# Two transformer blocks on one core: four edits to queues, buffers and engines at the seams between stages

## The chip, the core and the metric

The kernel runs on one core of one Trainium2 chip. Its engines have queues of their own, each worked off in order: TensorE (PE, the matmuls), VectorE (DVE), ScalarE (ACT), GpSimd (POOL) and SyncE (SP), which issues nearly all DMAs. The metric is the device time of one execution in microseconds (us), from the first instruction to the last.

## The reference

```python
def first_block(x, ...):                       # 1024 rows of 1024
    proj = rms_norm(x, norm1_g) @ w_in         # attention, convolution and pooling branches
    mix = concat([att(8 heads), conv, pool])
    x = x + mix @ w_out
    up = causal_depthwise_conv(rms_norm(x, norm2_g) @ w_up, ffn_dw_w)
    gate, val = split(up)                      # 2816 channels each
    return x + (silu(gate) * val) @ w_down

def second_block(x, ...):
    ...                                        # differential and neighbourhood attention, gates
    x = x + rmsnorm(merged @ w_out, post_mix_w)
    h = rmsnorm(x, pre_ffn_w)
    f = (silu(h @ w_gate) * (h @ w_up)) @ w_down
    return x + rmsnorm(f, post_ffn_w)

reference = second_block(first_block(x))       # all in float32
```

## The kernel before

All matmuls are float32 made from three passes: every operand is split into a high part (`hi`, a cast on ACT) and the rest (`lo`, a subtraction on DVE or POOL, `lo_of`), and a product is hi*hi + lo*hi + hi*lo. The feed-forward networks (FFN) use Strassen's scheme in a seven-product form. Going up (`ffn_up`), `T1` to `T7` are seven sums of quarters of the input, held in SBUF; each of 22 channel groups c has seven weight sums (A1 to A7) and seven products, whose PSUM tiles are named x, y and z. Channel groups come in pairs, and the seven sums of a finished pair are stored to DRAM (`gD`, 77 stores in each FFN). Going down (`ffn_down`), four groups of 2, 3, 3 and 3 pairs load these sums and the weight's quarters (11 loads of 256 KB for a pair), DVE makes the weight sums (L975), ACT and `lo_of` split (tiles `hl`), and seven products are added into eight rows.

The stages of the trace (us): the first mixing stage to about 474, `out1` (mix @ w_out) from 403 to 526, first way up 526 to 1012, first way down 1012 to 1240, second mixing stage, second `out` to 2192, second way up 2192 to 2656, second way down 2656 to 2886.

The code gives what is computed and from which buffers. The order on each engine comes from a list scheduler at build time with its own estimates of durations; a wait that turns out longer on the chip holds up all that stands behind it in that queue.

Places that the change touches. `attn_head` writes a head's output (`pvt`) to DRAM (`mixD`), and `out1` loads it back (`split_T`) and splits it as an operand `hA`, `hB`; the last pair of heads (`mixD[3]`) is read back last. The weights of `out1` (`wr<-in_w_out_dram`) and these loads share one tag of two buffers. In `ffn_up`, `weights_a` loads two 512 KB weight blocks for a channel group (tag `wr`, three buffers) and `weights_b` forms the other sums (`ws`); all split weights lie in tag `w`. `lo_of` gives a split to POOL and DVE in turn.

Of the kernel before, what the change touches and what calls it, by code (L numbers as in the profile page):

```python
# [11 lines left out]
F32R = mybir.dt.float32r  # L12
# [3 lines left out]
NOSYNC = mybir.DependencyInfo(mybir.DependencyClass.NoSync, mybir.DependencyReason.DATA)  # L16
# [4 lines left out]
P = 128  # L21
# [4 lines left out]
NF = DFF // P  # L26
# [55 lines left out]
class Net:  # L82
# [236 lines left out]

    def attn_head(self, st, V, lane, spans, in1, pool, ps, dst, causal=False):  # L320
        nc = self.nc
        for g in range(2):
            pv = ps.tile([P, 512], F32, tag="pv", name=self.n("pv"), bufs=1)
            for j in (2 * g, 2 * g + 1):
                ts = {}
                for qb in (2 * j, 2 * j + 1):
# [5 lines left out]
                    r = self.sm(1, "rs")  # L332
# [20 lines left out]
                for bk in banks:  # L353
# [13 lines left out]
                    for kb, qs in bk:  # L367
# [11 lines left out]
            nc.vector.tensor_tensor(out=tmp[lane:lane + 64, :], in0=pv[lane:lane + 64, :],  # L379
                                    in1=tmp[lane:lane + 64, :], op=ALU.add)  # L380
            nc.sync.dma_start(out=dst[lane:lane + 64, g * 512:(g + 1) * 512], in_=tmp[lane:lane + 64, :])

# [19 lines left out]
    def mix1(self, pb, pt):  # L402
# [17 lines left out]
        def att(pr, pb):  # L420
            for hh in range(2):
                h = 2 * pr + hh
                st = self.load_stacks(pb, qD[pr], kD[pr], hh * 64)
                V = pt.tile([P, NB, P], F32R, tag="V", name=self.n("V"))
                nc.sync.dma_start(out=V.bitcast(F32), in_=vD[h])
                cB = pb.tile([P, S], F32, tag="cB", name=self.n("cB"))
                nc.sync.dma_start(out=cB, in_=cumD[h].partition_broadcast(P))
                yield from self.attn_head(st, V, hh * 64, CAUSAL, lambda qb: lambda a, b: [(a, b, cB[:, a:b])],
                                          pt, ps, self.mixD[pr], True)

        gB = self.bcast_row(I["norm1_g"][0], pb, "cB", 2)
        with self.pool("p1a", side="right") as pa:
# [18 lines left out]
            for pr in range(4):  # L451
                f = chain(*fill[pr])
                for _ in att(pr, pb):
                    for _ in range(1):
                        next(f, None)
                    n += 1
                    while rate[pr] and n * rate[pr] >= 1:
                        n -= 1 / rate[pr]
                        next(bg, None)
                drain(f)  # L460
# [206 lines left out]
    def out1(self, rows, pp, done):  # L667

        nc, I = self.nc, self.I
        W = I["w_out"][0]  # L670
        mT = self.new_hT()
        ws = []
# [20 lines left out]
        for i in range(4):  # L693
            part(i, 1, w1[:6])
        self.split_T(self.mixD[3], mT, 3)
        gB, jk = (self.wpool.tile([P, D], F32, tag="wr", name=self.n("wr"), bufs=2) for _ in range(2))
# [70 lines left out]
    def ffn_up(self, T, fT, fw, R, ps, Wg, cg, Wu, cu, conv, gD, close_sums):  # L767
        nc = self.nc
        chans, raws, pts = {}, {}, {}
        G, V, b_ = R[0], R[1], R[2][:, :S]  # L770
        t1, t2, t3, s1, s2, s4 = (R[i][:, o:o + 512] for i, o in ((3, 0), (3, 512), (4, 0), (4, 512), (7, 0), (7, 512)))
# [3 lines left out]
        def split(raw, w):  # L775
            hi, lo = (fw.tile([P, 1024], F32R, tag="w", name=self.n("w"), bufs=11)[:, :w] for _ in range(2))
            nc.scalar.copy(out=hi, in_=raw)  # L777
            self.lo_of(lo, raw, hi)
            return [(hi[:, o:o + 512], lo[:, o:o + 512]) for o in range(0, w, 512)]

        def weights_a(c):

            r = [fw.tile([P, 2, 512], F32, tag="wr", name=self.n("wr"), bufs=3) for _ in range(2)]
            for t, W, col in ((r[0], Wg, cg + c * P), (r[1], Wu, cu + c * P)):
                nc.sync.dma_start(out=t.rearrange("p h (k m) -> p (h k) m", k=4),
                                  in_=W[:, col:col + P].rearrange("(k p) m -> p k m", p=P))
            A = chans[c] = {}
            A[1], A[2] = split(r[0].rearrange("p h x -> p (h x)"), 1024)
            raws[c] = r
# [56 lines left out]
        def finish(c):  # L846
# [15 lines left out]
            if c % 2:  # L862
                a11, a21, a12, a22 = gp[0][:, :512], gp[0][:, 512:], gp[1][:, :512], gp[1][:, 512:]
                nc.vector.tensor_tensor(out=s1, in0=a21, in1=a22, op=ALU.add)
                nc.vector.tensor_tensor(out=a21, in0=a11, in1=a21, op=ALU.subtract)
                nc.vector.tensor_tensor(out=s2, in0=s1, in1=a11, op=ALU.subtract)
                nc.vector.tensor_tensor(out=s4, in0=a12, in1=s2, op=ALU.subtract)
                for i, t in ((1, a11), (2, a12), (3, s4), (4, a22), (5, s1), (6, s2), (7, a21)):
                    nc.sync.dma_start(out=gD[c // 2, i - 1], in_=t)

        for c in (0, 1):
            weights_a(c)
        for i in (3, 4, 6, 7, 5):
# [67 lines left out]
    def ffn_down(self, acc, keep, gD, Wd, fx, fr, fh, ps, done):  # L941
# [16 lines left out]
        def load(ps_):  # L958
# [5 lines left out]
            for i, half in ((1, 0), (1, 1), (5, 0), (5, 1), (6, 0), (3, 1), (7, 0), (4, 0), (2, 1), (3, 0), (2, 0)):  # L964
                for p in ps_:
                    if half == 0:
                        nc.sync.dma_start(out=X[p][i][:, 0], in_=gD[p, i - 1])
                    else:
                        r, h = {1: (0, 0), 5: (0, 1), 3: (1, 1), 2: (1, 0)}[i]
                        r = (2 * p + r) * P  # L970
                        nc.sync.dma_start(out=X[p][i][:, 1], in_=Wd[r:r + P, h * 512:(h + 1) * 512])
            for p in ps_:
# [18 lines left out]
        assert p == np_  # L991
        loaded = load(groups[0])
        rest = list(range(NB)) if keep is not None else []
        for gi, grp in enumerate(groups):
# [4 lines left out]
            for i in DOWN:  # L999
                hl = []  # L1000
                for p in grp:
                    raw = loaded[p][i].rearrange("p a b -> p (a b)")
                    hi, lo = (fh.tile([P, 1024], F32R, tag="hl", name=self.n("hl"), bufs=12) for _ in range(2))
                    nc.scalar.copy(out=hi, in_=raw)  # L1004
                    self.lo_of(lo, raw, hi)
                    hl.append((hi, lo))
# [412 lines left out]
```

## Time and profile before

| | |
|---|---|
| time, median of 3 runs | 2899.86 us (2897.95 to 2903.76) |
| profiled execution | 2904.8 us, its span 2903.0 us |
| PE busy | 2709.1 us, 93% of the span |
| mean granted TensorE clock | 0.972 of full speed |
| DVE, ACT, POOL busy | 1791.7, 1195.8, 913.7 us |

Busy time is the union of an engine's instructions. PE carries the span; what it does not carry is waiting that lies at the seams between stages and once per channel group on the first way up. The clock is 1.0 at the higher of TensorE's two levels (2.4 GHz) and 0.5 at the lower (1.2 GHz).

### The profile page before, as it was taken

To read this page: it belongs to the slowest core of one execution; us is meant where nothing else is said; L and a number is where in the kernel's file an instruction comes from. 1 tells how busy PE (TensorE), PEld (TensorE's weight loads), DVE (VectorE), ACT (ScalarE), POOL (GpSimd) and SP (SyncE) were. 2 spreads that over 40 slices of the span, in tenths; PEclk is the share of its full clock that TensorE was granted. 3 is DMA by queue.
4 is the path that set the end of the run, shared out by engine and by line. 5 is a ranking of instruction groups with operands and counts; after the bars stand their busy time and mean duration, and the time that the engine had idled before them with its cause. 6 is when DMAs were issued, how large, how long until landed. Compare 5 with 4: busy or idle time off the path is not lost. (4 is left out here: it accounts for less than half of the span.)

```text
span 2903.0 us, 37142 instructions
## 1 busy us (share of the span) xinstructions
PE 2709.1 (93%) x13686; PEld 2265.8 (78%) x13686; DVE 1791.7 (62%) x2730; ACT 1195.8 (41%) x1879; POOL 913.7 (31%) x642
## 2 busy tenths in 40 slices
PE   7999898899999989999999999998997999998997
PEld 7799677677777768888888978886776788886786
DVE  4697664677776799845666533444427544555977
ACT  4344553344444443334445444544323433333333
POOL 3256431222222144531212253422422211123445
PEclk9999999999999989999999999999998999999999
DMA  5445451223322474155654394525422233336522
GB/s 167 132 119 145 130 189 64 80 73 102 98 96 86 141 264 157 46 193 157 174 159 124 106 225 128 138 81 170 143 90 87 79 103 106 105 102 222 204 87 97
DMA packets 318143, 375.08 MB, mean 129 GB/s; under 512 B 42692, under 2 KB 215168, under 8 KB 317448
## 3 DMA queue, kind: packets, MB, share of 16 engines
q1 hardware_dynamic: 317960, 372.70, 41.8%
q8 instruction: 108, 1.77, 0.3%
q14 instruction: 75, 0.61, 0.1%
HBM read 257.01 MB, written 115.61 MB: 128 GB/s over the span
## 5 line engine op out<-in xcount | busy, mean ns | idle before, releaser
L765 POOL TENSOR_TENSOR hl<-x,hl 128x1024 fp32r<-128x1024 f32 x77 | 220.1, 2873 | 270.1 <-ACT hl L1004 220.3
L139 POOL TENSOR_TENSOR wl<-wr,wh 128x1024 fp32r<-128x1024 f32 x73 | 186.6, 2558 | 349.7 <-ACT wh L138 314.9
L1004 ACT CAST hl<-x 128x1024 fp32r<-128x1024 f32 x154 | 153.1, 1049 | 230.1 <-PE x L118 127.0
L317 ACT ACTIVATE t<-t,mx 128x640 f32<-128x640 f32 (+3 forms) x192 | 172.8, 901 | 160.8 <-DVE mx L313 155.0
L118 PE MATMUL x<-hl,hl 128*128 128x512 f32 x704 | 218.0, 396 | 5.2 <-DVE hl L765 2.8
L765 POOL TENSOR_TENSOR w<-wr,w 128x1024 fp32r<-128x1024 f32 (+1 forms) x44 | 84.7, 1924 | 389.6 <-PE x L118 288.0
L118 PE MATMUL mm<-hA,wh 128*128 128x512 f32 x608 | 198.0, 400 | 4.6 <-ACT gs L1204 4.6
L765 POOL TENSOR_TENSOR w<-ws,w 128x1024 fp32r<-128x1024 f32 x44 | 107.8, 2450 | 298.1 <-issue 210.7
L118 PE MATMUL mm<-hB,wh 128*128 128x512 f32 x608 | 196.4, 397 | 1.0 <-ACT gs L1204 1.0
L118 PE MATMUL y<-hl,hl 128*128 128x512 f32 x528 | 167.6, 403 | 16.6 <-DVE hl L765 12.8
L365 DVE TENSOR_TENSOR pl<-tr,ph 128x512 fp32r<-128x512 f32 (+2 forms) x160 | 100.4, 634 | 123.1 <-DMA yD<-pvt 42.9
L334 POOL TENSOR_SCALAR t<-t,rs 128x640 f32<-128x640 f32 (+7 forms) x128 | 106.4, 838 | 204.8 <-DVE rs L333 175.1
L118 PE MATMUL mm<-wh,hB 128*128 128x256 f32 (+1 forms) x752 | 164.0, 306 | 4.1 <-ACT hB L180 4.1
L118 PEld LDWEIGHTS x<-hl,hl 128*128 128x128 f32 x704 | 134.3, 191 | 35.4 <-DVE hl L765 4.3
L118 PE MATMUL mm<-wh,hA 128*128 128x256 f32 (+1 forms) x704 | 150.7, 302 | 11.2 <-ACT hA L127 7.8
L777 ACT CAST w<-ws 128x1024 fp32r<-128x1024 f32 x88 | 92.6, 1053 | 127.3 <-PE x L118 103.3
L118 PE MATMUL x<-hl 128*128 128x512 f32 x352 | 137.1, 398 | 6.2 <-DVE r L985 6.1
L364 ACT CAST ph<-tr 128x512 fp32r<-128x512 f32 (+2 forms) x160 | 84.8, 542 | 139.1 <-PE tr L359 93.6
L118 PE MATMUL z<-T2h,w 128*128 128x512 f32 x352 | 120.0, 402 | 23.0 <-DVE r L814 21.3
L118 PEld LDWEIGHTS mm<-hA,wh 128*128 128x128 f32 x608 | 115.3, 191 | 29.1 <-ACT gs L1204 5.3
L118 PE MATMUL sc<-KH,QS 128*128 128x512 f32 (+1 forms) x320 | 125.9, 396 | 12.1 <-DVE mx L313 9.0
L765 DVE TENSOR_TENSOR hl<-x,hl 128x1024 fp32r<-128x1024 f32 x77 | 129.7, 1687 | 11.1 <-ACT hl L1004 10.8
(345 smaller groups left out, 7674.7 us busy)
## 6 DMA issues: line engine op xcount, KB each, us to landing
gD<-r SPq DMA_DIRECT2D x154, 256.0 KB, 2.5
x<-gD SPq DMA_DIRECT2D x154, 256.0 KB, 5.3
wr<-in_w_up_dram SPq DMA_DIRECT2D x66, 512.0 KB, 3.8
wr<-in_w_in_dram SPq DMA_DIRECT2D x50, 512.0 KB, 7.2
x<-in_w_down_dram SPq DMA_DIRECT2D x88, 256.0 KB, 3.8
wr<-in_w_gate_dram SPq DMA_DIRECT2D x22, 512.0 KB, 4.1
wr<-in_w_out_dram SPq DMA_DIRECT2D x16, 512.0 KB, 4.1
QS<-q2D SPq DMA_DIRECT2D x32, 256.0 KB, 5.4
```

The lines of the kernel that those rows point to most:

```text
L118: self.nc.tensor.matmul(out, lhsT, rhs, start=start, stop=stop, **kw)
L139: g = (lo_engine or nc.gpsimd).tensor_tensor(out=lo, in0=raw[:, :n], in1=hi.bitcast(F32), op=ALU.subtract)
L317: nc.scalar.activation(out=t[:, :nb * P], in_=t[:, :nb * P], func=AF.Exp, scale=-1.0, bias=m, accum_out=s)
L334: nc.gpsimd.tensor_scalar(out=t[:, :nb * P], in0=t[:, :nb * P], scalar1=r, scalar2=1.0, op0=ALU.mult, op1=ALU.mult)
L364: nc.scalar.copy(out=ph[:, :w], in_=tr[:, :w])
L365: nc.vector.tensor_tensor(out=pl[:, :w], in0=tr[:, :w], in1=ph[:, :w].bitcast(F32), op=ALU.subtract)
L765: return eng.tensor_tensor(out=lo, in0=raw, in1=hi.bitcast(F32), op=ALU.subtract)
L777: nc.scalar.copy(out=hi, in_=raw)
L1004: nc.scalar.copy(out=hi, in_=raw)
```

## The change

Five edits, the fourth of which isn't in its short name.

- The last pair of attention heads is not stored: `attn_head` splits its output straight into the operand `mT` (four splits of 64x512 on ACT and DVE in place of four stores, one load and a split of 128x1024). `mT` is allocated before that pair.
- The first two channel groups of each `ffn_up` load their weights from ACT's DMA queue, not SP's.
- The seven `gD` stores of the last pair are ordered behind the last weight load of the first way-down group (an order for the scheduler, not a wait).
- Tag `w` in `ffn_up` has 8 buffers, not 11.
- In the first way-down group, all `lo` splits go to DVE (`lo_of(..., 1)`), seven of them POOL's before.

```diff
-    def attn_head(self, st, V, lane, spans, in1, pool, ps, dst, causal=False):
+    def attn_head(self, st, V, lane, spans, in1, pool, ps, dst, causal=False, direct=None):
...
+            if direct is not None:
+                mT, k = direct
+                part = slice(lane, lane + 64)
+                self.split(tmp[part, :], mT[0][g][part, k, :], mT[1][g][part, k, :], nc.vector)
+                continue
             nc.sync.dma_start(out=dst[lane:lane + 64, g * 512:(g + 1) * 512], in_=tmp[lane:lane + 64, :])
...
-                                          pt, ps, self.mixD[pr], True)
+                                          pt, ps, self.mixD[pr], True, (self.mT, 3) if pr == 3 else None)
...
+                if pr == 3:
+                    self.mT = self.new_hT()
...
-        mT = self.new_hT()
+        mT = self.mT
...
-        self.split_T(self.mixD[3], mT, 3)
...
-            hi, lo = (fw.tile([P, 1024], F32R, tag="w", name=self.n("w"), bufs=11)[:, :w] for _ in range(2))
+            hi, lo = (fw.tile([P, 1024], F32R, tag="w", name=self.n("w"), bufs=8)[:, :w] for _ in range(2))
...
-        def weights_a(c):
+        def weights_a(c, queue=nc.sync):
...
-                    nc.sync.dma_start(out=gD[c // 2, i - 1], in_=t)
+                    d = nc.sync.dma_start(out=gD[c // 2, i - 1], in_=t)
+                    if c == NF - 1:
+                        self.late.append(d.ins)
...
         for c in (0, 1):
-            weights_a(c)
+            weights_a(c, nc.scalar)
...
-                        nc.sync.dma_start(out=X[p][i][:, 1], in_=Wd[r:r + P, h * 512:(h + 1) * 512])
+                        self.mark = nc.sync.dma_start(out=X[p][i][:, 1], in_=Wd[r:r + P, h * 512:(h + 1) * 512])
...
+        for ins in self.late:
+            self.tc.add_manual_dep(ins, self.mark.ins.name, NOSYNC, reason="late")
...
-                    self.lo_of(lo, raw, hi)
+                    self.lo_of(lo, raw, hi, 2 if gi else 1)
```

The scheduler answers these edits with new orders. Three places follow. First SP's queue at the end of the first attention, before (`wr` are weight blocks of `out1` or read-back parts of `mixD`, `r` the eight input rows of the residual):

```order
L663 DMA wr_4838<-mixD 128x1024
L135 DMA wr_4844<-in_w_out_dram 128x2x512
L381 DMA mixD<-pvt_4085 64x512
L572 DMA mixD<-mo_4015 128x512
L572 DMA mixD<-mo_4021 128x512
L425 DMA V_4525<-vD 128x1024
L381 DMA mixD<-pvt_4247 64x512
L572 DMA mixD<-mo_4027 128x512
L572 DMA mixD<-mo_4033 128x512
L663 DMA wr_4850<-mixD 128x1024
L663 DMA wr_4856<-mixD 128x1024
L678 DMA r_1041_4786<-in_x_dram 128x1024
```

The same place after the change; `wr_4848` is what `wr_4844` was, and `wr_4830` what was `wr_4826`, ten rows ahead of the first row above:

```order
L685 DMA r_1045_4794<-in_x_dram 128x1024
L685 DMA r_1046_4795<-in_x_dram 128x1024
L685 DMA r_1047_4796<-in_x_dram 128x1024
L685 DMA r_1048_4797<-in_x_dram 128x1024
L685 DMA r_1049_4798<-in_x_dram 128x1024
L685 DMA r_1050_4799<-in_x_dram 128x1024
L685 DMA r_1051_4800<-in_x_dram 128x1024
L685 DMA r_1052_4801<-in_x_dram 128x1024
L135 DMA wr_4830<-in_w_out_dram 128x2x512
L670 DMA wr_4836<-mixD 128x1024
L670 DMA wr_4842<-mixD 128x1024
L135 DMA wr_4848<-in_w_out_dram 128x2x512
```

The two weight blocks move from ahead of the last attention stores to behind the eight loads of 512 KB. The matmuls that need them move with them, from between the steps of the last heads to behind the last head.

Second, PE in the middle of the first way up (x, y, z are PSUM tiles, T1 to T7 the operands). Before, the product z of the next channel group begins between two others:

```order
L118 MATMUL y_6711<-T5h_5533,w_6697 128x512
L118 MATMUL y_6711<-T5l_5534,w_6697 128x512
L118 MATMUL y_6711<-T5h_5533,w_6698 128x512
L118 MATMUL z_6852<-T2h_4799,w_6828 128x512
L118 MATMUL z_6852<-T2l_4800,w_6828 128x512
L118 MATMUL x_6712<-T6h_5529,w_6697 128x512
L118 MATMUL x_6712<-T6l_5530,w_6697 128x512
L118 MATMUL x_6712<-T6h_5529,w_6698 128x512
```

After, it begins behind the last product of the channel group before:

```order
L118 MATMUL y_6581<-T3h_5523,w_6574 128x512
L118 MATMUL y_6581<-T3h_5523,w_6573 128x512
L118 MATMUL y_6581<-T3l_5524,w_6573 128x512
L118 MATMUL y_6581<-T3h_5523,w_6574 128x512
L118 MATMUL z_6850<-T2h_4807,w_6826 128x512
L118 MATMUL z_6850<-T2l_4808,w_6826 128x512
L118 MATMUL x_6849<-T1h_4805,w_6826 128x512
L118 MATMUL x_6849<-T1l_4806,w_6826 128x512
```

Two matmuls of z move ahead, from in front of the x with `T6` to behind the y with `T3`; the x with `T6` then stands right behind a product of the channel group before.

Third, POOL at the first way down. Before (the last two weight splits of the way up, then the seven `lo` splits of the first group, then the next group's first):

```order
L765 TENSOR_TENSOR w_8431<-wr_8426,w_8430 128x1024
L765 TENSOR_TENSOR w_8445<-ws_8435,w_8444 128x1024
L765 TENSOR_TENSOR hl_8672<-x_8623,hl_8671 128x1024
L765 TENSOR_TENSOR hl_8730<-x_8625,hl_8729 128x1024
L765 TENSOR_TENSOR hl_8792<-x_8627,hl_8791 128x1024
L765 TENSOR_TENSOR hl_8850<-x_8629,hl_8849 128x1024
L765 TENSOR_TENSOR hl_8886<-x_8631,hl_8885 128x1024
L765 TENSOR_TENSOR hl_8922<-x_8633,hl_8921 128x1024
L765 TENSOR_TENSOR hl_8958<-x_8635,hl_8957 128x1024
L765 TENSOR_TENSOR hl_9002<-x_8707,hl_9001 128x1024
```

After:

```order
L771 TENSOR_TENSOR w_8429<-wr_8424,w_8428 128x1024
L771 TENSOR_TENSOR w_8443<-ws_8433,w_8442 128x1024
L771 TENSOR_TENSOR hl_9000<-x_8705,hl_8999 128x1024
L771 TENSOR_TENSOR hl_9008<-x_8825,hl_9007 128x1024
```

The seven splits are gone from POOL, and DVE's queue has them between its subtractions (here its first twelve rows of that stage, where every second `hl` row was POOL's):

```order
L984 TENSOR_TENSOR x_8627<-x_8631,x_8623 128x512
L771 TENSOR_TENSOR hl_8674<-x_8622,hl_8673 128x1024
L984 TENSOR_TENSOR x_8628<-x_8632,x_8624 128x512
L861 SCALAR_TENSOR_TENSOR r_1051_4800<-r_1045_4794,fdw,r_1051_4800 128x1024
L984 TENSOR_TENSOR x_8623<-x_8623,x_8621 128x512
L984 TENSOR_TENSOR x_8624<-x_8624,x_8622 128x512
L861 SCALAR_TENSOR_TENSOR r_1051_4800<-r_1045_4794,fdw,r_1051_4800 128x1024
L984 TENSOR_TENSOR x_8625<-x_8631,x_8623 128x512
L984 TENSOR_TENSOR x_8626<-x_8632,x_8624 128x512
L771 TENSOR_TENSOR hl_8728<-x_8623,hl_8727 128x1024
L984 TENSOR_TENSOR x_8629<-x_8633,x_8625 128x512
L771 TENSOR_TENSOR hl_8732<-x_8624,hl_8731 128x1024
```

The first store of the last pair (r5, a11) moves too: on SP it stood ahead of the first group's last four weight loads and now stands behind them and behind two loads of sums.

## Rows read from the trace of the kernel before

**Rows 1.** Stretches: us of the stretch, busy of each engine (instructions), PEclk, DMA share, GB/s.

```profile
403.00:526.00 123.00, 114.03 (x584) 95.61 (x583) 63.51 (x110) 38.59 (x69) 23.03 (x25) 0.96 0.35 122
...
600.00:940.00 340.00, 322.70 (x1368) 255.34 (x1367) 244.31 (x257) 146.31 (x180) 80.22 (x34) 0.99 0.30 95
...
1012.00:1110.00 98.00, 80.82 (x310) 61.72 (x310) 91.81 (x83) 38.74 (x48) 41.84 (x15) 0.91 0.69 239
1110.00:1240.00 130.00, 130.00 (x576) 107.66 (x575) 111.13 (x111) 51.45 (x57) 70.73 (x31) 1.00 0.31 105
2192.00:2250.00 58.00, 41.79 (x183) 32.67 (x183) 42.97 (x55) 22.50 (x36) 14.53 (x11) 0.82 0.25 74
2250.00:2630.00 380.00, 378.84 (x1654) 309.47 (x1653) 187.21 (x236) 138.17 (x182) 73.86 (x40) 1.00 0.30 96
2656.00:2740.00 84.00, 71.34 (x285) 56.28 (x284) 80.21 (x76) 36.80 (x45) 45.08 (x14) 0.93 0.74 262
```

**Rows 2.** Timeline at the end of the last head: start, us, instruction [idle before].

```profile
476.99 0.34 SPq L663 DMA_DIRECT2D wr<-mixD  x1
...
480.41 0.62 ACT L127 CAST hA<-wr 128x512 fp32r<-128x512 f32 x1 [6.52 <-DMA wr<-mixD]
...
481.08 0.80 PE L118 MATMUL mm<-wh,hA 128*128 128x512 f32 x1 [7.81 <-ACT hA L127]
```

**Rows 3.** Timeline of SP's queue, 398 to 414.

```profile
404.59 5.21 SPq L678 DMA_DIRECT2D r<-in_x_dram  x8
```

**Rows 4.** DMA issues, 403 to 425: count, KB each, median us to landing.

```profile
r<-in_x_dram SPq DMA_DIRECT2D x8, 512.0 KB, 10.0
```

**Rows 5.** PE's waits, 600 to 940: us in total, times, longest.

```profile
PE z L118 <- DVE r L814: 16.6, 15, 1.9
```

**Rows 6.** Timeline of PE in one channel group of the first way up.

```profile
728.51 0.39 PE L118 MATMUL y<-T3h,w 128*128 128x512 f32 x1
...
741.27 0.50 PE L118 MATMUL x<-T6h,w 128*128 128x512 f32 x1
```

**Rows 7.** Groups of instructions, 1012 to 1056: busy us, mean ns, idle before.

```profile
L765 POOL TENSOR_TENSOR hl<-x,hl 128x1024 fp32r<-128x1024 f32 x7 | 19.4, 2777 | 46.3 <-ACT hl L1004 45.5 <-DMA x<-gD 0.8
...
L765 DVE TENSOR_TENSOR hl<-x,hl 128x1024 fp32r<-128x1024 f32 x7 | 12.9, 1836 | 0.0
L975 DVE TENSOR_TENSOR x<-x,x 128x512 f32<-128x512 f32 x16 | 12.8, 817 | 0.0
...
L854 DVE SCALAR_TENSOR_TENSOR r<-r,fdw,r 128x1024 f32<-128x1024 f32 x4 | 8.7, 2183 | 3.6 <-ACT r L852 3.6
...
L860 DVE TENSOR_TENSOR r<-r,r 128x1024 f32<-128x1024 f32 x1 | 3.4, 3423 | 0.0
L865 DVE TENSOR_TENSOR r<-r 128x512 f32<-128x512 f32 x1 | 2.9, 2873 | 0.0
```

**Rows 8.** Timeline of DVE in the same stage.

```profile
1015.94 0.68 DVE L975 TENSOR_TENSOR x<-x,x 128x512 f32<-128x512 f32 x1
1016.54 1.21 DVE L765 TENSOR_TENSOR hl<-x,hl 128x1024 fp32r<-128x1024 f32 x1
...
1018.88 1.27 DVE L854 SCALAR_TENSOR_TENSOR r<-r,fdw,r 128x1024 f32<-128x1024 f32 x1
```

**Rows 9.** Groups of instructions, 2656 to 2700.

```profile
L975 DVE TENSOR_TENSOR x<-x,x 128x512 f32<-128x512 f32 x16 | 21.5, 1359 | 0.2
...
L765 DVE TENSOR_TENSOR hl<-x,hl 128x1024 fp32r<-128x1024 f32 x8 | 13.1, 1644 | 0.8 <-ACT hl L1004 0.8
```

**Rows 10.** Timeline of SP at the start of the second way up.

```profile
2194.02 10.33 SPq L1299 DMA_DIRECT2D x3D<-r  x2
2204.66 0.38 SPq L785 DMA_DIRECT2D wr<-in_w_up_dram  x1
```

**Rows 11.** Timeline of ACT at the same place.

```profile
2204.07 1.06 ACT L186 ACTIVATE o<-r 128x1024 f32<-128x1024 f32 x1 [1.35 <-DVE r L1298]
```

**Rows 12.** Timeline of DVE at the same place.

```profile
2212.18 0.68 DVE L797 TENSOR_TENSOR ws<-wr 128x512 f32<-128x512 f32 x1
```

More of the change, by code (lines that the diff above doesn't have):

```diff
@@ L769, in ffn_up @@
         chans, raws, pts = {}, {}, {}
+        self.late = []
         G, V, b_ = R[0], R[1], R[2][:, :S]
@@ L779, in split @@
             return [(hi[:, o:o + 512], lo[:, o:o + 512]) for o in range(0, w, 512)]
-        def weights_a(c):
+        def weights_a(c, queue=nc.sync):
             r = [fw.tile([P, 2, 512], F32, tag="wr", name=self.n("wr"), bufs=3) for _ in range(2)]
             for t, W, col in ((r[0], Wg, cg + c * P), (r[1], Wu, cu + c * P)):
-                nc.sync.dma_start(out=t.rearrange("p h (k m) -> p (h k) m", k=4),
-                                  in_=W[:, col:col + P].rearrange("(k p) m -> p k m", p=P))
+                queue.dma_start(out=t.rearrange("p h (k m) -> p (h k) m", k=4),
+                                in_=W[:, col:col + P].rearrange("(k p) m -> p k m", p=P))
             A = chans[c] = {}
```

## The prediction

> **What bounds the kernel now.** Start with the shares: PE is busy for 2709.1 of 2903.0 us, so the whole stock of waiting is under 200 us, and only a change that shortens a wait of PE, or makes one, moves the time. Then ask for the busy time of each engine by stretch [rows 1] and read PE's column against the length. The reader is to see two kinds of stretch. In 1110 to 1240 and 2250 to 2630 PE has no room (130.00 of 130.00 and 378.84 of 380.00): nothing done there can gain. The other five hold the waits: 9.0 us around the first `out1`, 17.3 in 600 to 940 of the first way up, 17.2 and 12.7 where the ways down begin, 16.2 where the second way up begins. In these the granted clock is lower too (0.91, 0.82, 0.93): part of PE's busy time there ran at TensorE's lower level, 1.2 GHz, after the longer pauses. 576 matmuls in 130.00 us give 0.226 us for one at the higher level.
>
> Next ask what ends each wait. At 481.08 PE has stood for 7.81 us until the read-back last pair of heads was cast [rows 2]. On the first way up it is always product z waiting for a DVE addition that empties PSUM, 15 times, 16.6 us in all [rows 5]. At the ways down, DVE's groups show it: idle 0.0 before nearly every group, and means far above what the same instruction takes alone [rows 7, 8].
>
> **Direct hand-over.** It removes four stores, a load (issued at 476.99, cast at 480.41) and the 7.81 us that end there [rows 2]; the four new splits are of the size of the copies that they follow and lie beside PE's other work. But the order of SP shows a second effect: two weight blocks of `out1` now stand behind eight loads of 512 KB. Those are issued from 404.59 to 409.80 [rows 3] and take 10.0 us to land [rows 4], so the first block comes at about 420. The matmuls that used to fill PE between the steps of the last heads now run mostly behind them. I work out the new end of `out1`: first cast at 420; from there the read-backs and a second weight block pass the two buffers, each load with 3.4 us from issue to cast (476.99 to 480.41 [rows 2]) and its splits before the buffer is free, some three rounds of 5 to 7 us one behind the other: 17.6 us by my count, an estimate; then 180 matmuls of PE's new order at 0.226, 40.6; then what stood behind the wait before, 481.08 to 526, 44.9. The sum is 523.1, 2.9 us earlier than the 526 of before. If the heads without filler are slower than that and the first cast falls at 432, it is 9 us later; if nothing but PE's own work counts, the 9.0 us of waits go, less a pause, for 8 earlier. I take **-1** (-8 to +9), nearer to the worked sum but shaded towards the late end, since a head alone is a chain through four engines and nothing shows its length without filler.
>
> **Weights on ACT's queue.** At the second way up three loads of the first four went out by 2190 and the fourth stood behind two row stores, issued at 2194.02 and over 10.33 us, until 2204.66 [rows 10]. On ACT the fourth stands behind the last row's sum of squares, which ran from 2204.07 for 1.06 us [rows 11]: 2205.1, half a us later, not earlier. DVE, its first user, came to it at 2212.18 [rows 12], so either is early enough. By these rows the edit is worth nothing at this place, and the waits there, which DVE's row work ends, stay. The Trainium skill, "DMA: Bandwidth & Descriptors", section "Issuing engines are not separate DMA queues", says that transfers from either engine run on the same 16 DMA engines and that a second issuer saves only issue time: by that the gain is 0. The trace agrees as far as it goes, with 0.38 us for the fourth issue. A small reorder of DVE's work brings one split forward by about a us: I take **-1** (-3 to +1) for the second way up's start and 0 for the first.
>
> **Eight buffers in `w`.** They hold exactly one channel group's operands, so each split now waits for a product of the group before. In the second way up PE has no room [rows 1] and there is a channel's time between the two: 0. In the first, the order of PE changes: the x with T6, not z, is now the one that waits for DVE. Before, it was 12.4 us from the end of the y with T3 (728.51 + 0.39) to x with T6 (741.27) [rows 6]. The four products between are 48 matmuls, 10.8 us; if DVE's and ACT's chain allowed that, most of the 16.6 us [rows 5] would go. But the chain itself hasn't become shorter; the splits on POOL still hold up DVE in it. I count 0.2 us less for each of some 16 channel groups, **-3**, with the whole 16.6 as the best and +5 (0.3 for each) as the worst case.
>
> **Splits of the first group on DVE.** In 1012 to 1056 DVE works without a break and PE waits for it. Seven splits of 1.21 us alone [rows 8] are added: 8.5. Removed is the stretching by POOL. Its rows [rows 7] against the durations alone [rows 8]: the seven splits that DVE had, 12.9 - 7 x 1.21 = 4.4; sixteen subtractions, 12.8 - 16 x 0.68 = 1.9; four convolution steps, 8.7 - 4 x 1.27 = 3.6; the two single ones, 3.4 and 2.9 against 1.2 and 0.7 for instructions of their size, 4.4. That is 14.3, so DVE's queue ends 5.8 us earlier. I take **-6** (-11, when the lower clock goes as well, to 0). At the second way down the same sum is 21.5 - 10.9 plus 13.1 - 8 x 1.21, together 14.0 less 8.5, 5.5 [rows 9]; but DVE paused there at times and PE's order is mixed anew, so **-4** (-8 to +1). These durations are what speaks for the edit. Against it speaks the Trainium skill, "Perfetto Trace Analysis", section "Optimizing Scalar/DVE Operations": where DVE is saturated, moving work off it, even to GpSimd, may pay, though the two share a read port and it may not. DVE is saturated here, 91.81 of 98.00 us [rows 1], and the edit moves work to it; by the first half of that rule each way down would lose the 8.5 us, by the stretched rows it wins 5.8.
>
> **Late stores.** One store of seven moves by six places, behind four weight loads and two loads of sums: these go out up to 10 us earlier, and DVE's first subtraction, at 1015.94, was not held up by loads (no idle time stands at its row) [rows 8]. I take 0, included in the two ranges above; it is cover for DVE when that becomes faster.
>
> **The sum.** -1 -1 -3 -6 -4 = -15. On the profiled execution's own time of 2904.8 us that is 2889.8; this execution lay 4.9 us above the median, 2899.86, so on the median's scale 2884.9, and I write **2885**.
>
> **Rivals.**
> - *The wait in the first way up falls away.* With z moved, PE finds 10.8 us of work where 12.4 passed, and the chain may be shorter than it looks because its start waited for POOL. Then -16 in place of -3: 2872. For it: POOL's splits delay the chain by chance, not by need. Against: nothing removes an instruction from the chain.
> - *Given back in `out1`.* The heads without filler run late, first cast at 432: +9 in place of -1, and the way down gains half: +9 -1 -3 -3 -2 = 0, 2900. For it: a chain with nothing to hide it. Against: the loads land by 420.
> - *Eight buffers stall.* The cast of the next group's A1, A2 waits in ACT's queue for the x with T4 of the group before, and ACT's copies out of PSUM stand behind it, so PE waits at every channel group, 42 in both ways up. At 0.7 us each that is +29 in place of -3, with the rest -12: 2917. It decides from (12 + 6)/42 = 0.43 us each. For it: no spare buffer. Against: the operand is needed a product's length or more after it is freed.
> - *DVE is the bound.* As the rule above: each way down loses 8.5, +17 -1 -1 -3 = +12: 2912. It decides when less than about 3 of the 14 us of stretching come back. For it 91.81 of 98.00; against it the means of 1836 and 3423 ns.
>
> **How the numbers follow.** A measurement of this kernel tells about 0.2%, 6 us, from no change. My case, -6 to -30 by its terms, has 0.52; the long wait's end 0.20; no change 0.14; buffers 0.08; DVE 0.06. Faster 0.73 (0.52 + 0.20, with a little from the no-change case), same 0.14, slower 0.13. The range leaves out the two slow cases and the far end of the fast one: **2862 to 2901**; the likeliest case alone runs from 2874 to 2894.
>
> **What would show it.** Right: no wait before the first matmul of the last pair's operand; in the stage of the first way down no DVE subtraction above 1 us before the second group's splits, PE's waits there under 12 us; z's waits on the first way up gone and shorter ones at x with T6. Wrong: PE idle around 420 to 440, waits of PE or of ACT's casts once per channel group in 2250 to 2630, or DVE's queue ending later than 1056 with all its rows short.

## The result: 1.7% faster, over three times the predicted gain

| | before | after |
|---|---|---|
| time, median (4 runs each, same chip) | 2901.78 us (2897.95 to 2903.76) | 2850.24 us (2847.58 to 2857.7) |
| ratio, 95% interval | | 0.9828 (0.9806 to 0.985) |
| span of the profiled execution | 2903.0 us | 2848.2 us |
| mean granted TensorE clock | 0.972 | 0.978 |

The time lies 12 us below the range, 2862 to 2901. To see where it came from, cut the span of both profiles at the same points of the program: the first product of each way up and the first and last product of each way down, on PE.

| stretch | before | after | difference | predicted |
|---|---|---|---|---|
| to the first way up (attention, `out1`) | 529.4 | 529.1 | -0.3 | -1 |
| first way up | 482.9 | 451.9 | -31.0 | -3 |
| first way down | 237.3 | 225.0 | -12.3 | -6 |
| second mixer and row work | 946.5 | 947.0 | +0.5 | part of -1 |
| second way up | 459.4 | 461.4 | +2.0 | part of -1 |
| second way down | 230.3 | 216.3 | -14.0 | -4 |
| end | 17.2 | 17.5 | +0.3 | |

The stretches answering to [rows 1], in the same columns, in the changed kernel (each starts where the matching work starts now):

```profile
404.00:526.00 122.00, 112.11 (x548) 91.82 (x547) 66.16 (x108) 40.49 (x68) 26.07 (x25) 0.99 0.37 130
526.00:600.00 74.00, 62.75 (x283) 49.76 (x284) 48.20 (x62) 32.96 (x49) 16.19 (x9) 0.93 0.20 59
600.00:940.00 340.00, 340.00 (x1484) 277.19 (x1483) 275.12 (x284) 164.43 (x195) 112.81 (x36) 1.00 0.32 103
981.00:1079.00 98.00, 88.17 (x365) 70.17 (x366) 91.91 (x103) 43.90 (x52) 30.08 (x11) 0.97 0.74 260
...
2148.00:2216.00 68.00, 50.47 (x217) 38.98 (x215) 45.69 (x59) 24.66 (x40) 18.86 (x11) 0.82 0.26 77
2216.00:2590.00 374.00, 373.12 (x1629) 305.54 (x1628) 206.01 (x234) 134.10 (x177) 72.60 (x39) 1.00 0.30 99
2614.00:2702.00 88.00, 82.84 (x360) 66.96 (x359) 86.56 (x98) 42.52 (x51) 24.20 (x10) 1.00 0.76 272
```

Read PE's column against the length. In 600 to 940 PE now has no pause at all and does 1484 matmuls where it did 1368 in the same 340 us [rows 1]. At the two ways down its pauses are 9.8 and 5.2 us, from 17.2 and 12.7, and the clock is 0.97 and 1.00, from 0.91 and 0.93. Around `out1` the pauses are 9.9 us, from 9.0: nothing gained. The start of the second way up gained nothing: in 58 us that begin as far ahead of its first product as before (2149 to 2207) PE pauses for 16.4 us, from 16.2, at a clock of 0.79, from 0.82.

### What the first way up had been waiting for

In the kernel before, DVE's idle time in 600 to 920 has this as its largest entry (us in all, times, longest):

```profile
DVE ws L797 <- DMA wr<-in_w_up_dram: 48.6, 16, 4.4
```

It doesn't stand among the rows on which the prediction rests, and it is where the gain comes from, as experiment 3 shows below. DVE's timeline of one channel group of the kernel before shows what lay behind that wait:

```profile
726.06 1.23 DVE L765 TENSOR_TENSOR w<-ws,w 128x1024 fp32r<-128x1024 f32 x1 [4.30 <-PE x L118]
729.85 2.01 DVE L797 TENSOR_TENSOR ws<-wr 128x512 f32<-128x512 f32 x1 [2.56 <-DMA wr<-in_w_up_dram]
731.78 0.68 DVE L814 TENSOR_TENSOR r<-y,r 128x512 f32<-128x512 f32 x1
732.39 1.27 DVE L854 SCALAR_TENSOR_TENSOR r<-r,fdw,r 128x1024 f32<-128x1024 f32 x1
...
739.68 0.69 DVE L814 TENSOR_TENSOR r<-z,r 128x512 f32<-128x512 f32 x1
```

The product y with `T3` was done at 728.90 [rows 6]. The addition that empties it stood second in DVE's queue, behind the first weight sum of a later channel group (L797). That sum needed a weight block which SP had issued at 725.80, when POOL's split of an older block (723.37 for 2.40 us) had given back a `wr` buffer. So the y addition ran at 731.78, 2.9 us after its product, and with it came late the convolution steps and, at 739.68, the z addition, for which PE waits. The sum itself took 2.01 us, not 0.68, beside a split on POOL. The Trainium skill's "SBUF — State Buffer", section "Who interferes with whom", has the port pair that the two engines share as an exclusive lock. The rows agree: POOL's next split ran from 728.91 for 2.40 us, and the sum ended 0.55 us after it.

The same place after the change:

```profile
718.50 0.68 DVE L821 TENSOR_TENSOR r<-y,r 128x512 f32<-128x512 f32 x1
719.10 1.21 DVE L771 TENSOR_TENSOR w<-ws,w 128x1024 fp32r<-128x1024 f32 x1
720.24 2.47 DVE L861 SCALAR_TENSOR_TENSOR r<-r,fdw,r 128x1024 f32<-128x1024 f32 x2
722.63 0.68 DVE L804 TENSOR_TENSOR ws<-wr 128x512 f32<-128x512 f32 x1
723.23 1.27 DVE L861 SCALAR_TENSOR_TENSOR r<-r,fdw,r 128x1024 f32<-128x1024 f32 x1
724.43 0.68 DVE L805 TENSOR_TENSOR ws<-ws,wr 128x512 f32<-128x512 f32 x1
725.03 0.68 DVE L821 TENSOR_TENSOR r<-z,r 128x512 f32<-128x512 f32 x1
```

The weight sum (now L804) stands behind the y addition and finds its block there: no idle time is shown at it. From the y addition to the z addition it is 6.5 us, from 7.9. From the end of the product with `T3` (716.87 here) to the end of the z addition it is 8.8 us, from 11.5. In the order of weight sums and y additions on DVE the whole stage differs by one swap: before, a channel group's first weight sum stands just ahead of the y addition of the group three before; now it stands just behind it.

### How 16.6 us of waits became 31

PE's timeline of the kernel before, around the one wait of [rows 6]:

```profile
740.52 0.48 PE L118 MATMUL z<-T2h,w 128*128 128x512 f32 x1 [1.01 <-DVE r L814]
740.84 0.40 PE L118 MATMUL z<-T2l,w 128*128 128x512 f32 x1
...
741.60 0.40 PE L118 MATMUL x<-T6l,w 128*128 128x512 f32 x1
741.83 0.62 PE L118 MATMUL x<-T6h,w 128*128 128x512 f32 x2
```

From 740.52 to 741.83 PE starts four matmuls in 1.31 us; at 0.227 each they take 0.91. So each wait costs some 0.4 us more than the gap that the profile puts down to it. About 0.1 of it lies right behind the z, and 0.3 is a second wait, at the x with `T6` (741.27 [rows 6]). PE's own list doesn't have it; the list of its weight loads (PEld) in 600 to 920 does, and ACT's timeline shows the copy of x that it names:

```profile
PEld x L118 <- ACT r L820: 7.2, 15, 0.5
...
739.68 1.06 ACT L856 ACTIVATE r<-r 128x1024 f32<-128x1024 f32 x1 [4.50 <-DVE r L854]
740.65 1.05 ACT L820 COPY r<-x 128x512 f32<-128x512 f32 x2
```

The first of the two copies ends at about 741.2, and the x starts. The copy stands behind an activation that waited for DVE's last convolution step: the same late chain holds PE a second time, by way of ACT. Over the stretch 600 to 920 the windows show, of the kernel before:

```profile
600.00:920.00 320.00, 304.63 (x1298) 241.18 (x1297) 232.57 (x244) 137.60 (x169) 77.33 (x32) 1.00 0.30 97
```

and of the changed one:

```profile
600.00:920.00 320.00, 320.00 (x1397) 260.85 (x1396) 257.74 (x266) 155.01 (x183) 106.51 (x34) 1.00 0.32 101
```

That is 99 matmuls more in the same time, 22.7 us at 320/1397 each. PE's pauses of before are only 15.4 us of the stretch; the other 7.3, some 0.5 for each of the 14 waits that PE's list has there, lie in the starts behind them. Scaled from 320 to the 412 us that were left to the first way down, 22.7 becomes 29; the start of the stage, 283 matmuls for 276, adds 1.6. That makes 31, as an estimate.

### The profile page after: what moved, and what is told of

Same layout as the page of the kernel before. It is cut to its first block, busy times and chain, and to the rows that moved or that the text cites. A ratio compares the mean times of both kernels' runs of the same rounds, so it can differ in the third digit from the quotient of the medians.

```text
span 2848.2 us, 37041 instructions
## 1 busy us (share of the span) xinstructions
PE 2690.7 (94%) x13686; PEld 2263.1 (79%) x13686; DVE 1793.6 (63%) x2746; ACT 1200.8 (42%) x1879; POOL 893.9 (31%) x628
## 4 chain that ended last, share of the span: by engine, by line
PE 48%; DMA 6%; DVE 3%; POOL 2%; issue 2%; ACT 1%; SPq 1%; POOLq 0%; DVEq 0%; ACTq 0%
PE mm L118 17%; PE x L118 13%; PE y L118 7%; PE sc L118 4%; PE pv L118 3%; PE z L118 2%; PE tr L359 1%; PE tr L1089 1%; DVE x L984 1%; DMA wr<-yD 1%; DMA x<-in_w_down_dram 1%; POOL hl L771 1%; DMA k2D<-nh 1%; DVE r L994 1%; DMA x<-gD 1%
## 5 line engine op out<-in xcount | busy, mean ns | idle before, releaser
L771 POOL TENSOR_TENSOR hl<-x,hl 128x1024 fp32r<-128x1024 f32 x63 | 174.2, 2779 | 276.6 <-ACT hl L1015 148.5
L771 POOL TENSOR_TENSOR w<-ws,w 128x1024 fp32r<-128x1024 f32 x44 | 135.3, 3076 | 247.9 <-ACT w L784 247.9
L861 DVE SCALAR_TENSOR_TENSOR r<-r,fdw,r 128x1024 f32<-128x1024 f32 x88 | 122.2, 1405 | 72.2 <-ACT r L859 72.0
L118 PE MATMUL y<-hl,hl 128*128 128x512 f32 x528 | 161.7, 392 | 3.6 <-DVE hl L771 3.6
L784 ACT CAST w<-wr 128x1024 fp32r<-128x1024 f32 (+1 forms) x88 | 73.6, 838 | 216.4 <-PE x L118 125.7
L771 DVE TENSOR_TENSOR hl<-x,hl 128x1024 fp32r<-128x1024 f32 x91 | 142.9, 1576 | 10.3 <-ACT hl L1015 10.0
L827 ACT COPY r<-x 128x512 f32<-128x512 f32 x132 | 76.7, 581 | 144.8 <-PE x L118 86.9
```

The lines of the kernel that those rows point to most:

```text
L118: self.nc.tensor.matmul(out, lhsT, rhs, start=start, stop=stop, **kw)
L771: return eng.tensor_tensor(out=lo, in0=raw, in1=hi.bitcast(F32), op=ALU.subtract)
L827: nc.scalar.copy(out=snaps[j], in_=pts[c]["x"])
L861: nc.vector.scalar_tensor_tensor(out=t, in0=src[:, 2 - s:2 - s + S], scalar=self.fdw[:, 2 - s, cc:cc + 1], in1=t, op0=ALU.mult, op1=ALU.add)
```

## The experiments

All are built from the kernel before unless it says otherwise; `add_manual_dep` with NOSYNC sets an order on one engine and adds no wait. "First way up" and so on are the stretches of the table above, from the run's profile.

**1. Eight buffers alone.**

```diff
-tag="w", ... bufs=11)
+tag="w", ... bufs=8)
```

> Before, with tag w in 8 buffers and nothing else. If the order that this tag brings is the whole cause of the first way up: that stage 452 us (483.0 before), PE without a wait over 0.5 us between 600 and 920, the time about 31 us under before, 2870. If my prediction's size was right and another edit brought the rest: the stage at 480, the time 2899. The second way up is 459.3 before and 461.4 after the change: if the tag costs it, 461; if the queue does, 459.

Measured: 2872.89 us, ratio 0.9904 (0.9879 to 0.9928); first way up 457.3, PE busy 319.39 of 320.00 us in 600 to 920, the ways down as before (236.8, 230.2). The edit makes up most of the gain by itself, 29 us of 51.5. Its profile, of an execution 10.9 us above this median, has a span 21.4 us shorter than before, this stage 25.6 us shorter and no other shorter by more than 0.5.

**2. The splits alone.**

```diff
-                    self.lo_of(lo, raw, hi)
+                    self.lo_of(lo, raw, hi, 2 if gi else 1)
```

> Before, with the first way-down group's lo splits on DVE and nothing else. If the splits alone bring what the ways down gained: first 225 us (237.3 before, 225.0 after the change), second 216 (230.3 before, 216.3 after), the time about 26 us under before. If the stores ordered behind the loads bring half: 231 and 223, 13 us. If my predicted sizes hold, 231 and 226, 10 us.

Measured: 2884.26 us, 0.9932 (0.9913 to 0.9951); first way down 227.8 (-9.5), second 216.7 (-13.6), first way up unchanged (481.8). The two stretches of [rows 1] in this kernel, each at the same distance from its stage's first product, to within a us:

```profile
1011.00:1109.00 98.00, 86.36 (x353) 67.87 (x353) 92.80 (x101) 42.79 (x52) 25.65 (x10) 0.95 0.74 258
2648.00:2732.00 84.00, 78.64 (x341) 63.17 (x339) 82.41 (x93) 39.58 (x48) 23.31 (x9) 1.00 0.78 276
```

In the first, PE's pauses fell from 17.2 to 11.6 us. That is 5.5 less, near the predicted 5.8 of DVE's queue. But PE also did 43 matmuls more, 9.7 us at 0.226: a matmul took 86.36/353 = 0.245 us of its busy time, from 80.82/310 = 0.261, while the granted clock rose from 0.91 to 0.95. In the second the pauses fell by 7.3 (12.7 to 5.4) and a matmul went from 0.250 to 0.231, the clock from 0.93 to 1.00. The pauses don't account for 4.0 of 9.5 us and 6.3 of 13.6. By the granted clock alone, an estimate, a matmul would have come to 0.261 x 0.91/0.95 = 0.250 and 0.250 x 0.93/1.00 = 0.233: some two thirds of the first fall and nine tenths of the second. The rest wasn't followed up. The second way down came out 5 us shorter in experiments 3 and 10 too (225.3 and 225.2), whose edits don't touch it, so its 13.6 and the parts of it are good to some 5 us.

**3. Only the place of the weight sum.** Eleven buffers stay; in the first way up a channel group's first weight sum is ordered behind the y addition of the group two before.

```diff
+            if conv and c > 2:
+                self.tc.add_manual_dep(d.ins, self.yadd, NOSYNC, reason="behind y")
```

> Before, with 11 buffers in tag w; only on DVE the first weight sum of the next channel group is ordered behind the addition that empties the y tile (first way up alone; the scheduler moves other work as well, but the two matmuls of z stay in front of the x of the channel group, as before). Late weight sum as the cause: z's waits of 16.6 us in 600 to 940 go, the stage 452 to 456 us. PE's order as the cause (z moved behind the y with T3): the waits stay at 12 us or more, the stage 475 or more.

Measured: 2868.02 us, 0.9876 (0.9849 to 0.9904); first way up 451.0, no wait of PE in 600 to 920. The profiled execution lay 9.1 us below this median; of the 45.9 us that its span is shorter, 31.9 lie in this stage, 4.0 and 5.0 in two that the edit doesn't touch (up to the first way up, and the second way down). DVE's idle time at the weight sums is gone with it (DVE's waits, 600 to 920):

```profile
DVE r L856 <- ACT r L854: 55.3, 16, 6.3
DVE r L816 <- PE y L118: 11.4, 15, 0.8
...
```

PE's order of products isn't quite that of the kernel before (among others, the x with `T4` now precedes the x with `T6`), but the first two matmuls of z stand at the same distance behind the product with `T3`, 46 matmuls, and no longer wait. So neither fewer buffers nor the moved z is needed for the gain: the weight sum's place in DVE's queue, behind the y addition, is enough. (It stands a channel group later here than in the changed kernel.) Whether the moved z alone would have gained, no run tests. The rows of the kernel before speak against it, as an estimate: in the changed kernel the x with `T6` stands 48 matmuls behind the product with `T3`, so by the times of before it would be due at about 739.7, and ACT's copy of x ended at about 741.2. It would wait some 1.5 us where z waited 1.0.

**4. The late stores alone** (the two hunks with `self.late` and `self.mark`).

```diff
+        for ins in self.late:
+            self.tc.add_manual_dep(ins, self.mark.ins.name, NOSYNC, reason="late")
```

> Before, with the last pair's stores ordered behind the last weight load of the first way-down group and nothing else. As I took it in the prediction: both ways down within 1.5 us of before (237.3 and 230.3), the time the same. If the loads were what DVE lacked: 3 us or more shorter each.

Measured: 2900.73 us, 0.9993 (0.9981 to 1.0004): no change that can be told, as predicted. In its profile the ways down are 3.3 and 1.6 us shorter; other stretches took that back.

**5. The hand-over alone** (`direct`, `self.mT` before the last pair, no read-back of it).

```diff
-        self.split_T(self.mixD[3], mT, 3)
```

> Before, with the last pair of heads handed over on chip and nothing else. The wait of 7.81 us goes, but the filler moves behind the heads: from the start to the first matmul of the way up 529 us (529.4 before, 529.1 after the change), the time the same within 3 us. If the removed wait counts in full: 522 and 7 us under before. If the heads without filler run late: 538 and 9 over.

Measured: 2907.09 us, 1.0018 (1.0005 to 1.003); stretch to the first way up 526.9, 2.5 us shorter, and nothing of it left in the whole.

**6. ACT's queue alone.**

```diff
-            weights_a(c)
+            weights_a(c, nc.scalar)
```

> Before, with the first weight loads on ACT's queue and nothing else. By the trace of before the fourth load goes out no earlier: both ways up within 2 us of before (482.9 and 459.4), the time the same. If it is this edit that cost the second way up its 2 us after the change: 461 to 462 there. If it helps the first way up's start: 478 to 480 there.

Measured: 2908.53 us, 1.002 (1.001 to 1.003); second way up 460.0, from 459.4. No gain. The Trainium skill's "DMA: Bandwidth & Descriptors", section "Issuing engines are not separate DMA queues", has transfers of all issuers on the same 16 DMA engines, with only issue time to be saved; no gain fits that. Nor did the loads go out earlier on the whole. This execution is 3.7 us later at this place (the same activation of ACT starts at 2195.34, from 2191.67). With that taken off, ACT issued the first load, behind its own row work, 5.2 us later than SP had (2195.35, from 2186.46) and the fourth 0.5 us earlier (2207.83, from 2204.66 [rows 10]).

**7 and 8. Hand-over, late stores and splits, with the weight sum ordered as in 3 and eleven buffers; 8 has ACT's queue too.**

> Hand-over, late stores and splits on DVE as in the change, but 11 buffers in tag w with the first weight sum ordered behind the y addition, and all weight loads on SP. If the parts add up as measured alone: -34 for the order, -18 for the splits, about 0 for hand-over and stores, 2848 to 2851, the time of the change. If ACT's queue is what costs the second way up 2 us, 2846. If the parts interfere: above 2856.

> As the one before it, with the first weight loads on ACT's queue as well. Against it this shows that edit beside the others: 2 us slower if it costs the second way up, equal within 2 us if not.

Measured: 2850.76 us, 0.9826 (0.9806 to 0.9845), and 2851.76 us, 0.9831 (0.9812 to 0.985); first way up 452.2 and 452.4. The order of experiment 3 does all that the eight buffers do (after: 0.9828), and the queue makes no difference.

**9. The opposite order, on the changed kernel.**

```diff
+            if conv and c > 2:
+                self.tc.add_manual_dep(self.yadd.ins, d.ins.name, NOSYNC, reason="sum first")
```

> The changed kernel, all five edits and its eight buffers in w, with one order added in the first way up: on DVE the y addition of a channel group may not come before the first weight sum of the group after next (the order that the kernel before has). Theory A (in the kernel before, the weight sum that waits for its late load stood ahead of the y addition in DVE's queue; eight buffers only turned that order round): the waits come back although the buffers are eight: about 1 us or more at most channel groups, the stage of the first way up 465 to 485 us in place of 452, the whole 2863 to 2885. Theory B (eight buffers gain by themselves, because PE's order of products is another one or the weights are cast at another time): the stage stays at 450 to 456 and the whole at 2846 to 2858.

Measured: 2854.32 us, 0.9832 (0.981 to 0.9853); first way up 454.9, no waits. This run tells nothing: the expectation took the wrong channel group. In the kernel before, a sum stands ahead of the y addition of the group three before; the order asked for here, ahead of the one two before, is what the changed kernel has already, and its order on DVE didn't change.

**10. The place kept, the load earlier.** One of the eleven buffers of `w` goes to `wr`, nothing else.

```diff
-tag="w", ... bufs=11)
+tag="w", ... bufs=10)
-tag="wr", ... bufs=3)
+tag="wr", ... bufs=4)
```

> The kernel before with one of the eleven buffers of w given to wr instead (ten in w, four in wr), nothing else. On DVE every weight sum of the first way up keeps its place ahead of the y addition of the group three before, as in the kernel before; only the load that it waits for can go out a block earlier, since a fourth raw buffer is there. Theory A (the 48.6 us that DVE stood at 16 such sums for their loads, with the y addition queued behind, is what made PE wait): DVE's idle time at the sums falls to under 10 us, PE's waits for z go, the stage of the first way up falls from 482.9 to 450 to 458 and the whole to 2866 to 2878. Theory B (the place itself or the number of buffers in w decides, not the load): the stage stays at 475 to 485 and the whole within 6 us of before.

Measured: 2886.8 us, 0.9953 (0.9937 to 0.997); first way up 465.4. The sums stand ahead of the y additions as before, and DVE no longer waits for their loads (DVE's waits, 600 to 920):

```profile
DVE w L765 <- ACT w L777: 63.7, 16, 5.3
DVE r L860 <- ACT r L856: 6.8, 17, 0.4
```

PE's waits for z are gone too, and 17.5 us come back with every sum in its old place on DVE. But the run separates less than it was meant to: `w` lost a buffer, and PE's order changed with it. All twelve matmuls of z now stand right behind the product with `T3`, so z no longer asks for the addition where it did. What the earlier load does is read from DVE's chain instead. From the end of the product with `T3` to the end of the z addition it is 10.3 us here (median of 16 channel groups), from 11.5 before and against 8.8 in the changed kernel. In the kernel before z started 11.6 us behind that product, 1.0 of it waiting; with this chain it would hardly have waited there either. So of the 2.6 us by which eight buffers shorten the chain, some 1.2 come here with the load alone, in a kernel whose PE order is another one too. The size missed: 450 to 458 was expected. PE does 1368 matmuls in 600 to 920, from 1298 and against 1397 in the changed kernel, and its timeline there shows what is left:

```profile
717.85 0.39 PE L118 MATMUL x<-T7h,w 128*128 128x512 f32 x1
718.34 0.50 PE L118 MATMUL x<-T6h,w 128*128 128x512 f32 x1
718.67 0.39 PE L118 MATMUL x<-T6l,w 128*128 128x512 f32 x1
```

In this kernel's order the x with `T6` follows the x with `T7`, and starts 0.49 us after it where 0.227 is the step: some 0.26 us for every channel group. The rows of the weight loads, 600 to 920, name the wait:

```profile
PEld x L118 <- ACT r L820: 9.4, 17, 1.1
```

It is again ACT's copy of x, which here starts at 717.72, behind the activation that needs the last convolution step: the chain is shorter, but still longer than PE's 48 matmuls. Its first 74 us (526 to 600) also hold 252 matmuls, not 276. Why they do wasn't looked into further.

**11. Both first weight blocks of `out1` early,** on top of kernel 7.

```diff
-        for k in (0, 6, 4):
-            ws += self.pair(W, k, 0)
+        ws += self.pair(W, 0, 0)
+        ws += self.pair(W, 6, 0)
+        for k in (0, 6, 4):
+            if k == 4:
+                ws += self.pair(W, 4, 0)
```

> The earlier kernel with the hand-over, the late stores, the DVE splits and the weight sum ordered behind the y addition (eleven buffers, weights on SP's queue; 2850.8 us, first stage 530.3), and in out1 the first two weight blocks now both stand ahead of the read-backs of the other heads, so that both go out before the last attention pair. Theory A (the 7.81 us that the hand-over took away were given back because the second weight block of out1 came to SP only behind the x loads and after a buffer wait, so that PE had no out1 products to put between the steps of the last heads): the first stage falls to 520 to 526, the whole to 2840 to 2847. Theory B (the last heads are a chain of their own or the read-backs, which now come later, bound it): first stage 528 to 533, the whole 2848 to 2855.

Measured: 2858.23 us, 0.9842 (0.9828 to 0.9855); stretch to the first way up 537.2, 6.9 us longer than in kernel 7. Neither of the two expected numbers came. Both weight blocks went out ahead of the last heads, but SP's queue now stood for another reason, an output that ACT had not written yet (SP's waits, 390 to 440):

```profile
SPq L579 <- ACT mo L578: 15.3, 4, 11.9
...
```

The eight `x` loads behind it went out at 415.00, from 402.88 in kernel 7, and the whole end of the attention came later. So early weight blocks are not enough for a gain; why that output came late was not followed up.

**12. Kernel 7 without the hand-over.**

> The kernel before with the late stores, the DVE splits and the weight sum ordered behind the y addition, eleven buffers, without the hand-over and without ACT's queue. If the hand-over is worth -1 as predicted, 2851 to 2853; if it costs the 0.2% that it showed alone, 2843 to 2847 with a first stage of 526 to 530. By sums of stages measured apart: 529.4 + 451 to 452 + 225 + 947 + 460 + 217 to 219 + 17 = 2846 to 2850 of span.

Measured: 2854.25 us, 0.9828 (0.9814 to 0.9842); stretch to the first way up 529.4. With the hand-over (7) it was 0.9826 and 530.3, so the hand-over is worth nothing that can be measured. None of the twelve is measurably faster than the changed kernel.

## Why the prediction was right in sign and wrong in its largest term

**The step that failed** is the buffers' term: "But the chain itself hasn't become shorter; the splits on POOL still hold up DVE in it. I count 0.2 us less for each of some 16 channel groups, -3". It was -31. The chain that starts with the y addition did become shorter (from the end of the product with `T3` to that of the z addition 8.8 us, from 11.5), because its start had been held by a weight sum waiting for a load. Experiment 3 moves the sum and loses z's waits with z at the same distance on PE; experiment 10 brings the load earlier and shortens the chain with the sum in place. The prediction had looked at what PE waits for (a DVE addition) and at how long DVE's instructions take, but not at what DVE itself waits for in that stretch, where 48.6 us stood in one row. That the term had the right sign was luck: the swap of weight sum and y addition on DVE, which eight buffers bring, stands nowhere in it. The rival "the wait in the first way up falls away" had the right outcome and came near the reason: the chain's start did hang on POOL, but by way of the buffer that POOL's split gave back to the load (725.80 above), not by POOL's hold on DVE. Its price of -16 was too small: it counted the gaps in 340 us alone, without the starts behind them and without the rest of the stage. The waits at the x with `T6` that were to take z's place didn't come; in 600 to 920 of the changed kernel PE has none.

**The splits** had the right mechanism, and their terms were mis-sized: -6 and -4, measured apart -9.5 and -13.6. The count of DVE's queue was right for the first (5.8 predicted, 5.5 fewer us of pauses). What the term left to the far end of its range is the clock, the larger part of the rest by the estimate of experiment 2. The groups that answer to [rows 7], in the changed kernel (981 to 1025):

```profile
L771 DVE TENSOR_TENSOR hl<-x,hl 128x1024 fp32r<-128x1024 f32 x14 | 16.8, 1211 | 0.0
L984 DVE TENSOR_TENSOR x<-x,x 128x512 f32<-128x512 f32 x22 | 16.2, 753 | 0.0
L861 DVE SCALAR_TENSOR_TENSOR r<-r,fdw,r 128x1024 f32<-128x1024 f32 x4 | 5.1, 1276 | 4.2 <-ACT r L859 4.2
...
L867 DVE TENSOR_TENSOR r<-r,r 128x1024 f32<-128x1024 f32 x1 | 1.2, 1212 | 0.0
```

Splits of 1211 ns, from 1836, and convolution steps of 1276, from 2183, are the durations alone that the term used [rows 8]; the subtractions, 753 from 817, are close to theirs. In 44 us DVE now starts 14 splits where it started 7. The rival "DVE is the bound" is refuted in its price: DVE had more work, and both stages are shorter.

**The hand-over**, -1, came out at -0.3, for about the reason given. A single profile can't tell -0.3 from -1. The wait of 7.81 us is gone, and others stand in its place (PE's waits, 404 to 526, after):

```profile
PE tr L359 <- DVE pl L365: 4.1, 2, 2.7
PE mm L118 <- ACT hA L127: 1.7, 1, 1.7
...
```

The last heads' transposes wait for DVE's splits of the softmax rows, between 414 and 425, where `out1`'s matmuls used to stand. The text had expected the loads late; SP's timeline shows them:

```profile
402.58 3.87 SPq L685 DMA_DIRECT2D r<-in_x_dram  x8
417.62 0.38 SPq L135 DMA_DIRECT2D wr<-in_w_out_dram  x1
```

Between the two SP waited for a `wr` buffer, 11.1 us, until DVE had split an older read-back. The last heads have no other work beside them there; that this alone sets the stage is not shown, since experiment 11 moved the heads as well.

**ACT's queue and the late stores** were worth nothing that can be measured, from -1 and 0 predicted. The second way up's start has as much waiting as before (16.4 us, from 16.2); **eight buffers** stall nothing behind it, 373.12 of 374.00.

**The sum.** Measured one by one the edits give -29.0, -17.7, -1.2, +5.2 and +6.6: -36; together they give -51.5. Most of the 15 us between lies in the last two numbers, which don't hold beside the other edits: experiments 7, 8 and 12 put the queue and the hand-over at nothing. Without the two the sum is -48, and 3.6 us are left. Some of that is in the first way up: with eight buffers alone its first 74 us hold 270 matmuls at a clock of 0.86, with all edits 283 at 0.93, some 3 us. One profile of each doesn't settle more.

## What to carry to other kernels

When PE waits for an engine, ask next what that engine waits for in the same stretch: an in-order queue with a load's latency at its head delays everything behind it, and the row that names PE's wait shows only the last link. Look at the waits of PE's weight loads too: a second wait of the same chain stood there and in no row of PE. Price a regular short wait by the work done in a fixed stretch with and without it, not by the sum of its gaps. And where a saturated engine's instructions are stretched by a neighbour, taking the neighbour's share onto the engine can pay, and the granted clock may rise with the shorter pauses, as it did here.

## What the runs showed that was not expected

- A wait of about 1 us on PE went with a loss of some 1.5 us a channel group: 15.4 us of pauses stood for 22.7 us of work in 320 us, at a granted clock of 1.00 before and after. Some 0.3 us at each is a second wait, of a weight load for ACT.
- The stretch between the first way down and the second way up, whose end alone the queue edit reaches, took from 944.9 to 953.9 us in the profiles of the fourteen kernels. A single profile doesn't settle a stage's difference below some 5 us; the +0.2% of the hand-over and of the queue alone are of that size.
- On the first way down a matmul's share of PE's busy time fell from 0.261 to 0.245 us as the pauses were filled and the granted clock went from 0.91 to 0.95, with no matmul changed.
